# A planned order of instructions that begins earlier and ends later, with a cost model for shared transfers and engines

## The chip, the cores and the metric

The kernel runs on one core of a Trainium2 chip. The metric is the device time of one execution in microseconds (us), as the median of several runs. TensorE (PE) does the matrix products, VectorE (DVE), ScalarE (ACT) and GpSimd (POOL) the elementwise work, and SyncE (SP) issues most of the transfers between memory and the on-chip buffers. Every engine works through its own instructions in the order in which they stand in its program; an instruction that must wait holds up all that stand behind it on its engine. ScalarE issues some transfers too.

## The reference

Two layers over 1024 latent tokens and 256 context tokens of width 1024, in 32-bit floats, then a last RMSNorm. Layer 0 is windowed grouped attention (16 heads, 4 key/value heads, window 128) with a sink logit. Layer 1 is multi-head latent attention: queries from a low-rank projection cq, keys and values from a shared latent ckv, and a rotary part qr and kr. Both outputs are gated.

```python
for i in range(DEPTH):
    shift_x, scale_x, gate_x = adaln(c, ada_w[i], ada_b[i])
    hx = rms_norm(x, norm_g[i]) * (1.0 + scale_x[:, None]) + shift_x[:, None]
    if kind == 0:
        yx, yc = window_gqa(hx, hc, a_w_in[j], a_sink[j], a_w_out[j], ...)
    elif kind == 1:
        yx, yc = latent_attention(hx, hc, b_w_in[j], b_q_norm[j], b_w_uq[j], ...)
    x = x + gate_x[:, None] * yx
return rms_norm(x, final_g)

# in latent_attention
cq, ckv, kr, g = jnp.split(h @ w_in, [...], axis=-1)
q = (rms_norm(cq, q_norm) @ w_uq).reshape(b, n, B_HEADS, B_NOPE + B_ROPE)
kv = (rms_norm(ckv, kv_norm) @ w_ukv).reshape(b, n, B_HEADS, B_NOPE + B_V)
s = (einsum(qn, kn) + einsum(qr, kr)) * scale
yx = (softmax(s) @ v * jax.nn.silu(g)) @ w_out
```

## The kernel before

**Arithmetic.** A 32-bit product is made of three matmuls (`mm3`): each operand is split into a high part, which is a cast (L252), and a low part, which is the difference (L253); the products high-high, high-low and low-high are added in PSUM (L257 to L259). So a weight block reaches TensorE by four steps: a request by SyncE into a staging buffer (`stg`), the cast on ScalarE, the subtraction on VectorE or GpSimd, and the matmuls. Where the table of lines says L184, an instruction went through the recorder described below; its own line is lost.

**Stages.** First come the norms, the conditioning vectors (`AdaLN`, from `ada_w`) and the input projection of layer 0 in ten blocks of 256 columns, `proj_t(bi, gp, c)`, with block bi's weights fetched in four pieces by `fetch` (three at once, the fourth by `second`, since it reuses the first piece's staging buffer). The order within a block is gp 1, 2, 0. Beside the later blocks VectorE sums the products of `ada_w` piece by piece (L479), for the conditioning vectors that TensorE closes at L490. Then the attention of layer 0 runs over `units`. In some of its units (L1124) one of the ten x tiles of layer 1 (128 tokens by 1024, read from `x_d`) is loaded, squared for the norm and scaled ahead of time (`x1_load`, `x1_square`, `x1_scale` with L1093).

Then comes the passage to layer 1. Pairs of x tiles are transposed on TensorE (`turn1`, L1348), evacuated with scale and shift by ScalarE and VectorE (`h1_part`, L1355 and L1356), cast (`h1_top`, L1359) and subtracted (`h1_low`, L1363). Between them TensorE computes ckv and kr of each token tile (`kv_mm`, 288 columns); `kv_rstd` and `kv_post` norm and rotate it. `wq_cut` splits the weights of cq. `krF` holds the rotary keys.

Behind them stand the cq tiles (`cq_tile`, 512 columns in a single matmul each, but two halves in the first tile), then the rotary queries (`qr_tile`: the products on VectorE and GpSimd, their splits, a store), the other queries (`qn_tile`), the weights of keys and values and the gates (`g_tile`). Then the latent attention and the output projection.

**What sets the order.** Up to block 8 and from cq on, each engine's instructions stand in an order that the framework's own scheduler gives. In between, inside `tc.manual_schedule()`, they stand as the kernel emits them. There `Recorder` keeps every operation while `plan.on` is set, and `plan.emit()` puts them out by a list schedule: at each step the engine that can start an operation earliest takes, of its ready ones, that which stood first in the program. The times are those of `Plan.cost`, which gives every operation a duration on its engine and a latency for those who wait for it. Transfers are taken to be independent of one another, and VectorE and GpSimd not to disturb each other.

Of the kernel before, what the change touches and what calls it, by code (L numbers as in the profile page):

```python
# [61 lines left out]


class Plan:


    def __init__(self):
        self.ops = []
        self.on = False
        self.late = 0  # L70
        self.acc = {}

# [9 lines left out]
    @staticmethod  # L82
    def cost(eng, name, out, aps, k):
        n = out.free_size()
        psum = any(a.tensor.name.startswith("PB") for a in aps)
        if name == "dma_start":
            return 0.45, 2.4 + 4 * int(np.prod(out.shape)) / 385e3
        if eng == "tensor":
            return (0.108 if name == "transpose" else 0.0135 + n * 0.000417), 0.45
        if eng == "scalar":  # L90
            return 0.16 + n * 0.000857 + (0.12 if k.get("accum_out") is not None else -0.07 if n > 400 else 0), 0.34
        if eng == "gpsimd":
            if n < 8:
                return 0.59 if ALU.pow in k["alu"] else 0.21, 0.08
            return (0.18 + n * 0.00085 if "copy" in name else 0.19 + n * 0.00215), 0.08
        if name == "tensor_tensor_reduce":
            return 0.14 + n * 0.00105, 0.38
        if name == "reciprocal":
            return 0.1 + n * 0.0065, 0.17
        return (0.07 if psum else 0.03) + n * 0.00106, 0.37  # L100

    def add(self, eng, name, fn, a, k, line):
# [21 lines left out]
        func = a[2] if name == "activation" else None  # L124
        issue = FunctionType(at_line.__code__.replace(co_firstlineno=line), globals())
        self.ops.append((eng, dur, lat, deps, i + self.late, func, lambda: issue(fn, a, k)))

    def emit(self):
# [5 lines left out]
        ready, free, table, end = {}, {}, [None], [0.0] * n  # L134
        open_ = {}
        for i, o in enumerate(self.ops):
            if not left[i]:
                open_.setdefault(o[0], {})[i] = 0.0
        for _ in range(n):
            best = None  # L140
            for e, c in open_.items():
                if not c:
                    continue
                t = max(free.get(e, 0.0), min(c.values()))
                i = min((i for i, r in c.items() if r <= t), key=lambda i: self.ops[i][4])
                if best is None or t < best[0]:
                    best = (t, e, i)
            t, e, i = best
            del open_[e][i]
            _, dur, lat, _, _, func, fn = self.ops[i]  # L150
            if func in (AF.Exp, AF.Tanh, AF.Silu):
                kind = func == AF.Silu
                dur += 1.28 if table[0] not in (None, kind) else 0
                table[0] = kind
            fn()
            free[e] = t + dur
            for u in users[i]:
                left[u] -= 1
                x = t + dur + (0 if self.ops[u][0] == e and lat < 1 else lat)
                end[u] = max(end[u], x)  # L160
                if not left[u]:
                    open_.setdefault(self.ops[u][0], {})[u] = end[u]
# [4 lines left out]
class Recorder:  # L167
# [8 lines left out]
    def __getattr__(self, what):  # L176
# [3 lines left out]

        def call(*a, **k):
            if self.plan.on:
                return self.plan.add(self.name, what, fn, a, k, sys._getframe(1).f_lineno)
            return fn(*a, **k)  # L184

# [4 lines left out]
def kernel(ctx: ExitStack, tc: tile.TileContext, t, out, dbg=None):  # L190
# [842 lines left out]
    for bi, gp, c in order:  # L1033
        plan.on = plan.on or bi >= 8
        next_item()
# [62 lines left out]
    for ui, u in enumerate(units):  # L1098
# [14 lines left out]
        for ci in range(u.m):  # L1113
# [3 lines left out]
            if ci == 0:  # L1117
# [45 lines left out]
    qn = f_at(8, 512)  # L1163
    kvn = f_at(34, 256)
    stg = Ring(F, [30, 32, 64.25], 512)
# [251 lines left out]
    two = turn_two()  # L1417
    x1_square(4)
    h1_two(two)
    h1_two_out(two)  # L1420
    x1_square(5)
    x1_scale(4)
    x1_load(6)
    x1_load(7)
    for _ in last_outproj:
# [10 lines left out]
    for ti in range(NT):  # L1436
        h1_two(two)
        if ti < 5:
            x1_scale(ti + 5)
        if ti:  # L1440
# [3 lines left out]
        h1_two_out(now)  # L1444
        if ti < 4:
            x1_square(ti + 6)
        if ti:
# [56 lines left out]


    NU = 16
    Vq = f_at(34, NT, 4, 64)
# [434 lines left out]
```

## Time and profile before

| what | value |
|---|---|
| median of 3 runs | 1516.65 us (1516.38 to 1517.19) |
| the profiled execution | 1517.31 us |
| its span (first to last instruction) | 1515.5 us |
| granted TensorE clock, mean | 0.995 |
| moved by DMA | 178.93 MB, 118 GB/s |

The span is what the profiler saw on the core; the time of an execution has some 2 us more around it. The profile's page counts busy time of every engine; "idle before" is the time in which an engine stood ahead of an instruction, put down to the semaphore that came last. For an engine that is busy 98% of the time, the few waits are what an order can change.

### The profile page before, as it was taken

Reading aid. Unit: us, or ns where it says so; the run is one execution under the profiler, and the core shown is the slowest. Engines: PE = TensorE matmul, PEld = TensorE weight load, DVE = VectorE, ACT = ScalarE, POOL = GpSimd, SP = SyncE. Lnnn points to the kernel's source line nnn. Section 1 sums busy time; section 2 is a strip of 40 time slices with the busy share of each in tenths; the row PEclk is TensorE's granted clock in tenths of the full one; section 3 lists DMA queues with packets and bytes.
Section 4 is the critical chain, followed back from the end, with each engine's and each line's share of the span. In section 5 each row is a group of like instructions: output and inputs, shape, how many; then the busy total and the mean of one; then the engine's idle time right before and its main releaser. Section 6 shows DMA issues by size and latency. Waiting matters only on the chain.

```text
span 1515.5 us, 24962 instructions
## 1 busy us (share of the span) xinstructions
PE 1483.0 (98%) x9138; PEld 1200.5 (79%) x9138; DVE 954.5 (63%) x1871; ACT 710.3 (47%) x1363; POOL 818.4 (54%) x739
## 2 busy tenths in 40 slices
PE   6999999999999999998999999999999999999998
PEld 4888888788888888888887888677777767876687
DVE  4697689638778888878445103576466556565744
ACT  4421212259888888875333421354345434443422
POOL 2463265346454444456236420588789788789100
PEclk9999999999999999999999999999999999999999
DMA  9555654754343333343125831402212121111442
GB/s 335 162 186 165 192 184 137 235 176 115 122 150 123 93 95 90 95 130 126 43 70 211 258 94 62 113 15 60 63 46 67 46 77 60 46 50 42 156 151 84
DMA packets 128339, 178.93 MB, mean 118 GB/s; under 512 B 11980, under 2 KB 80716, under 8 KB 128216
## 3 DMA queue, kind: packets, MB, share of 16 engines
q1 hardware_dynamic: 123960, 170.93, 36.0%
q10 hardware_dynamic: 4256, 6.40, 1.2%
q8 instruction: 72, 1.18, 0.3%
q14 instruction: 51, 0.42, 0.1%
HBM read 131.13 MB, written 46.15 MB: 117 GB/s over the span
## 4 chain that ended last, share of the span: by engine, by line
PE 48%; POOL 2%; issue 1%; DVE 1%; ACT 0%; DMA 0%; ACTq 0%; POOLq 0%; DVEq 0%
PE PB L184 47%; POOL arena_f L184 1%; DVE arena_f L184 0%; DMA arena_f<-b_w_uq 0%; POOL arena_r L184 0%; ACT arena_f L184 0%; ACT arena_r L184 0%; DVE arena_r L184 0%; DVE arena_r L1363 0%; PE PB L259 0%; PE PB L257 0%; PE PB L258 0%; ACT arena_f L1355 0%; DVE arena_f L1219 0%; ACT arena_f L1186 0%
## 5 line engine op out<-in xcount | busy, mean ns | idle before, releaser
L184 PE MATMUL PB<-arena_r 128*128 128x512 f32 (+4 forms) x5296 | 843.8, 368 | 6.1 <-POOL arena_r L184 3.5
L184 PEld LDWEIGHTS PB<-arena_r 128*128 128x128 f32 (+2 forms) x5296 | 729.3, 187 | 121.8 <-issue 15.9
L184 POOL TENSOR_TENSOR arena_f<-arena_f 128x1024 f32<-128x1024 f32 (+2 forms) x205 | 423.9, 2068 | 147.7 <-ACT arena_f L184 90.5
L184 ACT ACTIVATE arena_f<-PB 128x1024 f32<-128x1024 f32 (+2 forms) x194 | 184.8, 953 | 244.5 <-PE PB L184 237.2
L184 DVE TENSOR_REDUCE krF<-PB 128x1 f32<-128x512 f32 (+1 forms) x324 | 205.9, 680 | 90.9 <-PE PB L184 90.9
L184 POOL TENSOR_TENSOR arena_r<-arena_f,arena_r 128x512 fp32r<-128x512 f32 x93 | 125.7, 1365 | 120.8 <-ACT arena_r L184 117.2
L676 DVE CUSTOM_DVE_ANT_0 arena_f<-PB,arena_f,small 128x256 f32<-128x256 f32 (+1 forms) x288 | 148.1, 525 | 54.5 <-PE PB L670 36.3
L184 PE MATMUL PB<-arena_f 128*64 128x512 f32 x640 | 145.9, 595 | 0.0
L682 ACT ACTIVATE arena_f<-arena_f,small 128x640 f32<-128x640 f32 (+2 forms) x160 | 119.1, 745 | 19.4 <-DVE small L676 17.8
L257 PE MATMUL PB<-arena_r 128*128 128x512 f32 (+2 forms) x336 | 125.3, 373 | 2.8 <-ACT arena_r L252 2.8
L253 DVE TENSOR_TENSOR arena_r<-PB,arena_r 128x512 fp32r<-128x512 f32 (+1 forms) x176 | 116.9, 673 | 15.6 <-ACT arena_r L252 15.0
L258 PE MATMUL PB<-arena_r 128*128 128x512 f32 (+2 forms) x336 | 122.4, 364 | 0.9 <-POOL arena_r L253 0.8
L259 PE MATMUL PB<-arena_r 128*128 128x512 f32 (+2 forms) x336 | 122.1, 363 | 0.0
L184 DVE SCALAR_TENSOR_TENSOR arena_f<-arena_f,small 128x512 f32<-128x512 f32 x100 | 109.8, 1148 | 16.2 <-POOL small L184 14.2
L709 PE MATMUL PB<-arena_r 128*128 128x512 f32 x336 | 118.7, 430 | 0.0
L252 ACT CAST arena_r<-PB 128x512 fp32r<-128x512 f32 (+1 forms) x176 | 99.6, 572 | 31.5 <-PE PB L699 29.9
L699 PE MATMUL PB<-ident,arena_f 128*128 128x128 f32 x672 | 108.5, 272 | 0.1
L184 PEld LDWEIGHTS PB<-arena_f 128*64 128x64 f32 x640 | 44.0, 137 | 79.6 <-issue 79.0
L184 ACT CAST arena_r<-arena_f 128x512 fp32r<-128x512 f32 (+1 forms) x111 | 67.0, 619 | 80.8 <-DVE arena_f L184 35.0
L699 PEld LDWEIGHTS PB<-ident,arena_f 128*128 128x128 f32 x672 | 83.9, 140 | 14.7 <-DVE arena_r L253 0.3
L669 PE MATMUL PB<-arena_r 128*128 128x256 f32 (+1 forms) x288 | 85.3, 312 | 0.3
L184 POOL TENSOR_TENSOR small<-small 128x1 f32<-128x1 f32 (+1 forms) x28 | 14.0, 499 | 130.4 <-ACT arena_f L184 66.9
(127 smaller groups left out, 1576.5 us busy)
## 6 DMA issues: line engine op xcount, KB each, us to landing
arena_f<-ada_w SPq DMA_DIRECT2D x96, 256.0 KB, 3.8
arena_r<-q_d SPq DMA_DIRECT2D x160, 128.0 KB, 2.9
arena_f<-a_w_in SPq DMA_DIRECT2D x40, 256.0 KB, 4.4
arena_f<-x SPq DMA_DIRECT2D x16, 512.0 KB, 6.5
q_d<-arena_f SPq DMA_DIRECT2D x16, 512.0 KB, 2.7
qn_d<-arena_f SPq DMA_DIRECT2D x16, 512.0 KB, 4.8
arena_r<-qn_d SPq DMA_DIRECT2D x16, 512.0 KB, 7.0
arena_f<-b_w_in SPq DMA_DIRECT2D x24, 256.0 KB, 3.1
```

Source lines behind the costliest of these rows:

```text
L184: return fn(*a, **k)
L252: nc.scalar.copy(hi, src)
L253: (lo_eng or nc.vector).tensor_sub(lo, src, hi.bitcast(F32))
L257: nc.tensor.matmul(o, ah, bh, start=first, stop=False)
L258: nc.tensor.matmul(o, al, bh, start=False, stop=False)
L259: nc.tensor.matmul(o, ah, bl, start=False, stop=last)
L669: nc.tensor.matmul(S, q[:, 0], kT[:, g, ko : ko + n], start=True, stop=False)
L676: nc.vector.tensor_tensor_reduce(o, S, mk, -A_SCALE, prev, ALU.add, ALU.min, mx)
L682: nc.scalar.activation(P, P, AF.Exp, bias=nm, scale=-1.0, accum_out=self.den[:, h : h + 1])
L699: nc.tensor.transpose(pt[:, h, :], self.Ps[h][:, ci * 128 : ci * 128 + 128], ident)
L709: nc.tensor.matmul(self.pv, V[:, self.chunks[ci], self.g, :], PT[:, s], start=ci == 0 and s == 0, stop=ci == self.m - 1 and s == 1,)
```

## The change

- The plan begins at `(bi, gp, c) == (9, 1, 1)`, behind the last requests for `a_w_in`, where it began with block 8.
- `plan.emit` stands behind the gates of layer 1, where it stood ahead of cq. So cq, qr, qn, the weights of keys and values and the gates are put in the planned order too. There a TensorE operation may run at most 40 recorded operations ahead of the first one not yet placed (`plan.reach`).
- The times: transfers share one clock (`dma`), each taking its bytes at 385 GB/s plus fixed parts; elementwise operations of VectorE and GpSimd on on-chip buffers slow each other by fixed rates; a SyncE operation that follows another one waits for its latency too.
- Five x tiles are fetched in the attention instead of four (units 24, 27, 30, 33, 36), with other buffers; squares and scalings of the rest move up by one tile.
- The last cq tile is computed in two halves of 256 columns, the second half first.
- An operation that is not planned keeps its own line number as well.

```diff
@@ Plan.cost
-            return 0.45, 2.4 + 4 * int(np.prod(out.shape)) / 385e3
+            return 0.45, 4 * int(np.prod(out.shape)) / 385e3
@@ Plan.add
+        heavy = eng in ("vector", "gpsimd") and "tensor_" in name and "copy" not in name and out.free_size() >= 128
+        heavy = heavy and not any(x.tensor.name.startswith("PB") for x in aps) and (2 if "scalar" in name else 1)
@@ Plan.emit
+                if e == "tensor":
+                    while first < n and (first in done or self.ops[first][0] != e):
+                        first += 1
+                    c = {i: r for i, r in c.items() if i <= first + self.ops[i][7]}
...
+            if e in ("vector", "gpsimd") and func:
+                rate = 0.7 if e == "gpsimd" else 0.35 if func == 1 else 0.65
+                both = max(0.0, big.get("gpsimd" if e == "vector" else "vector", 0.0) - t)
+                dur = min(dur / rate, both + max(0.0, dur - both * rate))
+                big[e] = t + dur
+            if e == "sync" or lat > 0.5:
+                dma = max(dma, t + dur + 1.4) + lat
+                lat = dma + 0.6 - t - dur
...
-                x = t + dur + (0 if self.ops[u][0] == e and lat < 1 else lat)
+                x = t + dur + (0 if self.ops[u][0] == e != "sync" and lat < 1 else lat)
@@ the kernel
-        plan.on = plan.on or bi >= 8
+        plan.on = plan.on or (bi, gp, c) == (9, 1, 1)
...
-    xr = Ring(F, [48, 52, 56, 60, 48, 52, 40, 44, 56, 60], 1024)
-    junk = f_at(36, 512).bitcast(BF16)
+    xr = Ring(F, [48, 52, 56, 60, 34, 48, 40, 44, 56, 60], 1024)
+    junk = f_at(64, 512).bitcast(BF16)
...
-                if ui in (24, 28, 32, 36):
-                    i = ui // 4 - 6
+                if ui in (24, 27, 30, 33, 36):
+                    i = ui // 3 - 8
...
-        for c in range(2) if ti == 0 else (slice(0, 2),):
-            o = ps[:, c * 256 : c * 256 + 256] if ti == 0 else shp(ps, 2, 256)
+        for c in {0: (0, 1), 7: (1, 0)}.get(ti, (slice(0, 2),)):
+            o = ps[:, c * 256 : c * 256 + 256] if ti in (0, 7) else shp(ps, 2, 256)
...
-    x1_load(4)
-    x1_load(5)
+    for i in (5, 6, 7):
+        x1_load(i)
...
-        if ti < 5:
-            x1_scale(ti + 5)
+        if ti < 4:
+            x1_scale(ti + 6)
...
-    plan.emit()
-    in_order.__exit__(None, None, None)
...
+    plan.reach = 40
     for ti in range(8):
         cq_tile(ti)
...
+    plan.emit(tensor=5.0)
+    in_order.__exit__(None, None, None)
```

The code before the planner's new lines is longer by 19 lines at its head, so a line behind it stands 19 lower in the new kernel, up to L1250 or so. Three places of the orders follow, each as it was and as it is.

SyncE's queue at block 9 (`a_w_in` are the projection's weights, `ada_w` the conditioning weights, `g0_d` stored gates), before:

```order
L420 DMA arena_f_65<-a_w_in 128x2x256 x3
L455 DMA arena_f_65<-ada_w 128x512 x2
L469 DMA arena_f_65<-ada_b 1x512
L770 DMA arena_f_65<-a_w_out 128x512
L455 DMA arena_f_65<-ada_w 128x512
L770 DMA arena_f_65<-a_w_out 128x512 x2
L1044 DMA arena_f_65<-mask 128x384
L455 DMA arena_f_65<-ada_w 128x512
L652 DMA arena_f_65<-g0_d_70 128x2x128
L420 DMA arena_f_65<-a_w_in 128x2x256
```

and now:

```order
L439 DMA arena_f_65<-a_w_in 128x2x256 x4
L474 DMA arena_f_65<-ada_w 128x512 x6
L488 DMA arena_f_65<-ada_b 1x512
L474 DMA arena_f_65<-ada_w 128x512 x2
L789 DMA arena_f_65<-a_w_out 128x512 x5
L474 DMA arena_f_65<-ada_w 128x512 x2
L1063 DMA arena_f_65<-mask 128x384
```

The fourth piece of the weights stands directly behind the first three; the ten other requests that stood ahead of it come after it.

VectorE in the passage to layer 1 (L1088 and L1093 are the norm and the scaling of an x tile, L756 and L757 the last rows of layer 0, L1356 the evacuations, L1363 the low halves), before:

```order
L1093 TENSOR_SCALAR arena_f_65<-arena_f_65,small_67 128x1024
L1356 TENSOR_SCALAR arena_f_65<-PB_63,small_67 128x256 x2
L1088 TENSOR_SCALAR small_67<-small_67 128x1 x2
L756 TENSOR_TENSOR arena_f_65<-PB_63,arena_f_65 128x512
L757 TENSOR_TENSOR arena_f_65<-arena_f_65 128x512
L1363 TENSOR_TENSOR arena_r_64<-arena_f_65,arena_r_64 128x512
L756 TENSOR_TENSOR arena_f_65<-PB_63,arena_f_65 128x512
L757 TENSOR_TENSOR arena_f_65<-arena_f_65 128x512
L1356 TENSOR_SCALAR arena_f_65<-PB_63,small_67 128x256 x2
L1093 TENSOR_SCALAR arena_f_65<-arena_f_65,small_67 128x1024
L1363 TENSOR_TENSOR arena_r_64<-arena_f_65,arena_r_64 128x512
L1093 TENSOR_SCALAR arena_f_65<-arena_f_65,small_67 128x1024
```

and now:

```order
L1112 TENSOR_SCALAR arena_f_65<-arena_f_65,small_67 128x1024
L1375 TENSOR_SCALAR arena_f_65<-PB_63,small_67 128x256 x2
L1107 TENSOR_SCALAR small_67<-small_67 128x1
L775 TENSOR_TENSOR arena_f_65<-PB_63,arena_f_65 128x512
L776 TENSOR_TENSOR arena_f_65<-arena_f_65 128x512
L1382 TENSOR_TENSOR arena_r_64<-arena_f_65,arena_r_64 128x512
L775 TENSOR_TENSOR arena_f_65<-PB_63,arena_f_65 128x512
L776 TENSOR_TENSOR arena_f_65<-arena_f_65 128x512
L1375 TENSOR_SCALAR arena_f_65<-PB_63,small_67 128x256 x2
L1112 TENSOR_SCALAR arena_f_65<-arena_f_65,small_67 128x1024
L1382 TENSOR_TENSOR arena_r_64<-arena_f_65,arena_r_64 128x512
L1107 TENSOR_SCALAR small_67<-small_67 128x1
```

The rows look alike, but the tiles differ: the scalings are those of tiles 4, 5 and 6 before and of tiles 5 and 6 now, since tile 4 is done in the attention.

GpSimd at the rotary queries (128x512 rows into `arena_f` are the rope's products and sums, those into `arena_r` low halves of weights), before:

```order
L184 COPY arena_f_65<-krF_68 128x256
L184 TENSOR_TENSOR arena_f_65<-arena_f_65 128x512 x6
L184 TENSOR_TENSOR arena_r_64<-arena_f_65,arena_r_64 128x512
L184 TENSOR_TENSOR arena_f_65<-arena_f_65 128x512
L184 TENSOR_TENSOR arena_r_64<-arena_f_65,arena_r_64 128x512
L184 TENSOR_TENSOR arena_f_65<-arena_f_65 128x512
L184 TENSOR_TENSOR arena_r_64<-arena_f_65,arena_r_64 128x512
L184 TENSOR_TENSOR arena_f_65<-arena_f_65 128x512 x2
L184 TENSOR_TENSOR arena_r_64<-arena_f_65,arena_r_64 128x512 x21
```

and now (L1301 is the product, L1302 the sum):

```order
L1301 TENSOR_TENSOR arena_f_65<-arena_f_65 128x512
L1302 TENSOR_TENSOR arena_f_65<-arena_f_65 128x512
L1301 TENSOR_TENSOR arena_f_65<-arena_f_65 128x512
L1302 TENSOR_TENSOR arena_f_65<-arena_f_65 128x512
L272 TENSOR_TENSOR arena_r_64<-arena_f_65,arena_r_64 128x512 x24
L1555 COPY arena_f_65<-krF_68 128x512
```

The three low halves that stood between the last rope operations now come behind all of them.

More of the change, by code (lines that the diff above doesn't have):

```diff
@@ L61, with at @@
 at_line = lambda fn, a, k: fn(*a, **k)
+def at(line):
+    return FunctionType(at_line.__code__.replace(co_firstlineno=line), globals())
 class Plan:
@@ L70, in __init__ @@
         self.late = 0
+        self.reach = 10 ** 6
         self.acc = {}
@@ L124, in add, with emit @@
         func = a[2] if name == "activation" else None
-        issue = FunctionType(at_line.__code__.replace(co_firstlineno=line), globals())
-        self.ops.append((eng, dur, lat, deps, i + self.late, func, lambda: issue(fn, a, k)))
-    def emit(self):
+        heavy = eng in ("vector", "gpsimd") and "tensor_" in name and "copy" not in name and out.free_size() >= 128
+        heavy = heavy and not any(x.tensor.name.startswith("PB") for x in aps) and (2 if "scalar" in name else 1)
+        self.ops.append((eng, dur, lat, deps, i + self.late, func or heavy, lambda: at(line)(fn, a, k), self.reach))
+    def emit(self, **free):
         n = len(self.ops)
@@ L133, in emit @@
                 users[j].append(i)
-        ready, free, table, end = {}, {}, [None], [0.0] * n
-        open_ = {}
+        table, end, big, dma = None, [0.0] * n, {}, 0.0
+        open_, done, first = {}, set(), 0
         for i, o in enumerate(self.ops):
@@ L149, in emit @@
             del open_[e][i]
-            _, dur, lat, _, _, func, fn = self.ops[i]
+            done.add(i)
+            _, dur, lat, _, _, func, fn, _ = self.ops[i]
             if func in (AF.Exp, AF.Tanh, AF.Silu):
-                kind = func == AF.Silu
-                dur += 1.28 if table[0] not in (None, kind) else 0
-                table[0] = kind
+                dur += 1.28 if table not in (None, func == AF.Silu) else 0
+                table = func == AF.Silu
+            if e in ("vector", "gpsimd") and func:
[6 more added lines that the diff above has]
+                lat = dma + 0.6 - t - dur
             fn()
@@ L181, in call @@
         def call(*a, **k):
+            line = sys._getframe(1).f_lineno
             if self.plan.on:
-                return self.plan.add(self.name, what, fn, a, k, sys._getframe(1).f_lineno)
-            return fn(*a, **k)
+                return self.plan.add(self.name, what, fn, a, k, line)
+            return at(line)(fn, a, k)
         return call
@@ L1163 @@
     qn = f_at(8, 512)
-    kvn = f_at(34, 256)
+    kvn = f_at(66, 256)
     stg = Ring(F, [30, 32, 64.25], 512)
@@ L1417 @@
     two = turn_two()
-    x1_square(4)
+    x1_square(5)
     h1_two(two)
     h1_two_out(two)
[L1421 to L1424, printed above, removed]
+    x1_square(6)
+    x1_scale(5)
     for _ in last_outproj:
@@ L1444 @@
         h1_two_out(now)
-        if ti < 4:
-            x1_square(ti + 6)
+        if ti < 3:
+            x1_square(ti + 7)
         if ti:
```

## The prediction

> **What bounds the kernel now.** I read the page first (busy times, granted clock), then the table of waits for TensorE alone, then busy time by stage, then the timeline at each stage where TensorE stands.
>
> ```profile
> span 1515.5 us, 24962 instructions
> PE 1483.0 (98%) x9138; PEld 1200.5 (79%) x9138; DVE 954.5 (63%) x1871; ACT 710.3 (47%) x1363; POOL 818.4 (54%) x739
> ```
>
> TensorE's own matmuls set the end: of the span only 1515.5 − 1483.0 = 32.5 us are left. A change of order can win no more than its share of these, plus whatever a lowered clock costs. The table of TensorE's waits says whom it stands for (us in total, times, longest):
>
> ```profile
> PE PB L1348 <- DVE arena_f L1093: 4.0, 3, 2.4
> ...
> PE PB L257 <- ACT arena_r L252: 2.8, 1, 2.8
> PE PB L184 <- DVE arena_f L184: 1.8, 2, 1.6
> PE PB L184 <- DVE arena_r L184: 1.5, 2, 0.8
> PE PB L1348 <- ACT arena_f L1355: 1.3, 1, 1.3
> ```
>
> Waits in the opening are left out here; they lie ahead of the point from which the new order reigns. These rows belong to three places, which the busy times by stage show (columns: window, its length, then busy time and count of PE, PEld, DVE, ACT, POOL, granted clock, DMA share, GB/s):
>
> ```profile
> 275.00:295.00 20.00, 16.28 (x57) 12.13 (x56) 13.49 (x14) 6.12 (x11) 6.33 (x5) 0.83 0.93 304
> 295.00:676.00 381.00, 380.63 (x2325) 333.46 (x2324) 282.96 (x862) 299.99 (x722) 183.90 (x325) 1.00 0.39 117
> 676.00:735.00 59.00, 53.47 (x384) 50.41 (x383) 46.68 (x106) 33.16 (x80) 37.41 (x44) 1.00 0.39 133
> 776.00:826.00 50.00, 47.62 (x216) 38.93 (x215) 28.51 (x47) 15.98 (x29) 33.20 (x26) 1.00 0.47 157
> 826.00:1497.00 671.00, 670.31 (x4347) 503.37 (x4346) 355.38 (x507) 264.50 (x351) 422.13 (x232) 1.00 0.29 87
> ```
>
> TensorE idles 3.7 us of 275 to 295 (the last projection block), 5.5 of 676 to 735 (the passage to layer 1) and 2.4 of 776 to 826 (cq to qr to qn). In the attention (295 to 676) it idles 0.4 and behind 826 only 0.7 in 671: there nothing is to be won. So the change is worth what it does at three places, and can cost wherever its order makes TensorE wait anew.
>
> **Place 1: the weights of block 9.** The timeline at 267 to 293 (start, length, engine; in brackets the idle time ahead and its releaser):
>
> ```profile
> 267.14 1.45 SPq L420 DMA_DIRECT2D arena_f<-a_w_in  x3
> 280.66 0.50 SPq L420 DMA_DIRECT2D arena_f<-a_w_in  x1
> 276.08 1.41 POOL L253 TENSOR_TENSOR arena_r<-arena_f,arena_r 128x512 fp32r<-128x512 f32 x1 [6.06 <-ACT arena_r L252]
> 284.54 0.62 ACT L252 CAST arena_r<-arena_f 128x512 fp32r<-128x512 f32 x1 [6.88 <-DMA arena_f<-a_w_in]
> 285.24 1.27 POOL L253 TENSOR_TENSOR arena_r<-arena_f,arena_r 128x512 fp32r<-128x512 f32 x1 [4.35 <-ACT arena_r L252]
> 281.99 0.40 PE L259 MATMUL PB<-arena_r 128*128 128x512 f32 x1
> 285.21 0.50 PE L257 MATMUL PB<-arena_r 128*128 128x512 f32 x1 [2.83 <-ACT arena_r L252]
> 287.15 0.63 PE L259 MATMUL PB<-arena_r 128*128 128x512 f32 x1
> 292.63 0.40 PE L257 MATMUL PB<-arena_r 128*128 128x512 f32 x1
> 286.00:287.00 1.00, 0.44 (x1) 0.44 (x2) 1.00 (x1) 0.00 (x0) 0.51 (x1) 0.50 0.73 230
> DMA to landing us min/median/max: 2.7/4.4/7.9
> ```
>
> Three of the four weight pieces are requested at 267.14, the fourth at 280.66, behind ten other loads in SyncE's queue. It lands at 284.54, ScalarE casts it, POOL makes its low half by 286.51, and TensorE stands. Then the granted clock is 0.50 until 292.3. Between 282.22, when the matmul that began at 281.99 gives way at the undisturbed pace of 0.227 us (12 matmuls from the one listed at 287.15 take 5.1 us at half clock, 0.427 each), and 292.63, fifteen matmuls run. At full pace they take 15 × 0.227 = 3.4; they took 10.4. **The place costs 7.0 us.**
>
> In the new order the fourth request stands directly behind the other three. It reuses the staging buffer of the first piece, so it must wait for POOL's low half of that piece, 276.08 + 1.41 = 277.5, and everything behind it in SyncE's queue waits too. It then goes out at about 277.6, 3.1 us earlier. With the 3.9 us from request to landing that the old one took it lands at 281.5, the cast ends 282.15, the low half 283.45. TensorE needs the high half at 282.2 and the low half at 282.45, so 1.0 us of waiting is left, and no half clock behind it, since the 2.43 us stall of place 2 left the clock at 1.00. Gain 7.0 − 1.0 = 6.0. At the shortest landing of any a_w_in load (2.7 us) nothing waits: 7.0. At the median (4.4) the low half is ready at 283.95: 5.5. The queue is empty by then, which speaks for less than 3.9: I take **6.3**, bounds 5.0 and 7.0.
>
> [...]
>
> What the held queue delays: eight ada_w pieces, the mask, a_w_out, each some 5 us. Their users on VectorE end 18.4 us ahead of the next work there, which waits for TensorE's use of the result:
>
> ```profile
> 313.61 1.40 DVE L495 TENSOR_TENSOR arena_f<-PB,arena_f 1x512 f32<-1x512 f32 x2 [18.42 <-PE PB L490]
> ```
>
> A delay of 5 is hidden three times over. Cost 0; without that cover it would be 5.
>
> **Place 2: the passage to layer 1.**
>
> ```profile
> 685.00:710.00 25.00, 21.98 (x168) 20.99 (x166) 23.70 (x46) 14.90 (x34) 18.91 (x19) 1.00 0.44 146
> 682.40 0.76 DVE L1093 TENSOR_SCALAR arena_f<-arena_f,small 128x1024 f32<-128x1024 f32 x1 [0.66 <-POOL small L1089]
> 690.78 0.99 DVE L1356 TENSOR_SCALAR arena_f<-PB,small 128x256 f32<-128x256 f32 x2
> 691.69 0.74 DVE L1093 TENSOR_SCALAR arena_f<-arena_f,small 128x1024 f32<-128x1024 f32 x1
> 692.49 0.88 PE L1348 MATMUL PB<-ident,arena_f 128*128 128x128 f32 x6 [2.43 <-DVE arena_f L1093]
> 696.76 0.68 DVE L253 TENSOR_TENSOR arena_r<-arena_f,arena_r 128x512 fp32r<-128x512 f32 x1
> 703.08 1.38 DVE L253 TENSOR_TENSOR arena_r<-arena_f,arena_r 128x512 fp32r<-128x512 f32 x1
> 710.33 0.74 DVE L1093 TENSOR_SCALAR arena_f<-arena_f,small 128x1024 f32<-128x1024 f32 x1
> 715.91 0.17 DVE L184 MEMSET krF<- 128x128 f32 x1 [1.61 <-POOL arena_f L184]
> ```
>
> VectorE is the engine here: of 685 to 710 it is busy 23.7 us of 25. TensorE's transposes (L1348) wait for the scaling of the next x tile (L1093), which stands behind evacuations (L1356) and weight splits (L253): the three waits of 4.0 us in the table; the 1.3 us there is the evacuation pair behind a MEMSET of krF that waits 1.6 us for POOL.
>
> The change takes one x tile out of this stretch (it is loaded, squared and scaled in the attention, where TensorE idles 0.4 of 381 us and VectorE has a quarter free): 0.75 us of VectorE. The scaling of tile 5 moves from 691.69 to the place that tile 4's had at 682.40. Behind the last scaling go two of the four splits of cq weights (0.68 and 1.38), the scaling of qn and the MEMSET. Together some 2.8 us of VectorE's work, qn not counted, leave the part in which TensorE waited 4.0 us.
>
> By stall: at 692.49 the scaling is no longer late, but the next evacuation is (the first of the pair at 690.78 ends about 691.3, TensorE comes there about 690.1): 2.4 becomes 1.1, gain 1.3. The other two share the remaining 1.6 of that row: the first (0.6) gives way to an evacuation (0.54, half of the pair's 0.99 and a little), gain 0.1; the second (1.0, for the scaling at 710.33) goes, since that scaling now stands ten places earlier. The 1.3 goes with the MEMSET. Sum 3.8. Lower bound: only the MEMSET's 1.3 is won, less 0.3 for an evacuation that splits now delay; upper: all 5.5 idle less 0.5. I take **3.8**, bounds 1.0 and 5.0.
>
> **Place 3: cq, qr, qn.**
>
> ```profile
> 779.98 0.62 ACT L184 CAST arena_r<-arena_f 128x512 fp32r<-128x512 f32 x1 [1.89 <-DMA arena_f<-b_w_uq]
> 783.46 0.65 PE L184 MATMUL PB<-ident,arena_f 128*128 128x128 f32 x4 [0.82 <-DVE arena_r L184]
> 319.22 0.28 PE L669 MATMUL PB<-arena_r 128*128 128x256 f32 x1
> 319.34 0.28 PE L670 MATMUL PB<-arena_r 128*128 128x256 f32 x1
> 814.27 1.30 POOL L184 TENSOR_TENSOR arena_r<-arena_f,arena_r 128x512 fp32r<-128x512 f32 x1
> 821.08 6.19 PE L184 MATMUL PB<-arena_r 128*128 128x512 f32 x26 [1.56 <-DVE arena_f L184]
> ```
>
> At 783.46 TensorE waits because ScalarE's square of the last cq tile stood behind a cast that waited for a transfer. In the new order the square comes first: 0.8 gained. At 821.08 it waits because VectorE's evacuations of qn stand behind the last rope pair, which stood on POOL behind three weight splits of 1.29; now all rope pairs come first: of 1.6 I take 1.4. The last cq tile is now computed in two halves: 24 matmuls of 512 columns become 48 of 256, nearest rows 319.22 and 319.34 (0.12 apart): 48 × 0.12 = 5.8 against 24 × 0.227 = 5.5, **+0.3**. Sum 0.8 + 1.4 − 0.3 = **1.9** gained, bounds −0.3 and 2.1.
>
> Attention and everything behind 826: order almost unchanged, 0; the new order there could cost up to 1.
>
> **Sum:** 6.3 + 3.8 + 1.9 = 12.0 us. The profiled execution took 1517.31 us (span 1515.5 and 1.8 around it), so 1505.3; it lies 0.66 over the median of the runs shown, 1516.65, so for the median **1504.6**.
>
> **The rivals.**
>
> *VectorE stays the bound in the passage.* What it has to do there is mostly the same; if each wait only turns from a scaling into an evacuation, place 2 gives 0. For it: 23.7 of 25 us busy. Against it: 2.8 us leave. Then 1516.65 − 6.3 − 1.9 = 1508.4.
>
> *The fourth piece lands no earlier.* It is 3.1 us earlier in the queue, and a_w_in loads took up to 7.9 us. At 7.9 it lands at 285.5, as late as now, and place 1 gives nothing: 1510.9. For it: the DMA share is 0.93 in this window. Against it: the loads that filled it stand behind now.
>
> *The clock falls all the same.* A remaining wait near 1 us does little, but if the clock falls for 6.4 us as it did (15 matmuls at 0.427, thus 3.0 lost), 1507.6. For it: the fall came only 0.7 us after the end of an idle stretch of 3 us, so what it counts is not seen. Against it: 2.43 us did nothing at 692.49. [...]
>
> *Slower: SyncE's queue held up in the passage.* The second b_w_uq request now stands ahead of the last x tile's load, and must wait for a staging slot that tile 4's transposes read. That slot comes free about 690. Should it come free only with later transposes, the last x tile comes late: now its load goes out at 695.56 and its scaling is at 710.33.
>
> ```profile
> 695.56 0.42 SPq L1083 DMA_DIRECT2D arena_f<-x_d  x1
> ```
>
> Between request and scaling lie 14.8 us today; a landing of 4.4 (the median quoted for weights), the square and the scaling need some 7, so up to about 703 a delay is free; from there each us costs one, and from 715 on all 12 are eaten. With the slot free at 725, 22 us are lost: 1516.65 − 12 + 22 = 1526.7. Against it: the addresses put the slot's last reader at 690.
>
> *It does nothing measurable:* the moved instructions all sat under waits whose true releaser is another; 1516.
>
> **How the numbers follow.** Chances: the forecast 0.48, VectorE still the bound 0.20, the piece no earlier 0.12, the clock 0.07, nothing 0.06, slower 0.07. What can be told from no change here is 0.2%, 3.0 us: faster 0.87, same 0.06, slower 0.07. The likeliest case by its bounds: 1516.65 − (7.0 + 5.0 + 2.1) = 1502.6 at best, and 1507.4 with places 1 and 2 at 5.5 and 1.9. The range takes in the rivals on that side: **1501 to 1511.5**.
>
> **What would show it.** Right: no wait of TensorE over 1.5 us between 275 and 300 and the granted clock 1.00 there; the transposes' waits (L1348 now) 2 us or less in total; none on VectorE's evacuation at the head of qn; TensorE's idle time down by 9 and its busy time down by 3. Wrong: 0.50 in the clock at 285; a wait for a DMA of a_w_in above 2 us; new waits of TensorE in 735 to 925; an idle SyncE queue in the passage while the last x tile is missing.

## The result and the profile after

The new kernel takes 1503.15 us in the median (1502.81 to 1503.98, 4 runs) against 1516.92 for the one before in the same runs: 0.991 of the time, 95% interval 0.9893 to 0.9927, or 13.8 us less. The profiled execution took 1503.46 us. The page of its profile:

```profile
span 1501.7 us, 24996 instructions
PE 1480.1 (99%) x9162; PEld 1201.6 (80%) x9162; DVE 954.0 (64%) x1871; ACT 708.8 (47%) x1363; POOL 820.1 (55%) x739
```

The span shrank by 13.8 us. TensorE's busy time fell by 2.9, although it runs 24 matmuls more: the half clock at block 9 is gone (the stage's mean was 0.83 before and is 1.00 now). Its idle time fell from 32.5 to 21.6. By stage (the same columns as before; the windows are moved to where the same work lies now):

```profile
275.00:292.00 17.00, 16.95 (x75) 13.51 (x74) 11.30 (x13) 4.64 (x9) 5.98 (x4) 1.00 0.67 233
292.00:668.00 376.00, 375.63 (x2302) 329.23 (x2301) 285.87 (x861) 299.99 (x724) 184.85 (x326) 1.00 0.41 124
668.00:724.00 56.00, 54.84 (x398) 52.65 (x397) 46.53 (x109) 33.10 (x82) 38.10 (x44) 1.00 0.43 147
765.00:815.00 50.00, 49.70 (x235) 41.33 (x234) 31.24 (x50) 18.57 (x34) 38.30 (x29) 1.00 0.61 215
815.00:1484.00 669.00, 668.31 (x4338) 502.01 (x4337) 353.25 (x503) 260.92 (x345) 418.19 (x230) 1.00 0.27 83
```

TensorE idles 0.05 us at block 9 where it idled 3.7, 1.2 in the passage where it idled 5.5, and 0.3 between cq and qn where it idled 2.4. What is left over in the table of its waits:

```profile
PE PB L830 <- DMA arena_f<-ada_w: 8.0, 2, 7.5
PE PB L897 <- POOL arena_r L883: 2.8, 2, 2.4
PE PB L1367 <- DVE arena_f L1375: 1.2, 1, 1.2
...
PE PB L1624 <- DVE arena_r L272: 0.7, 1, 0.7
...
PE PB L277 <- DVE arena_r L272: 0.3, 1, 0.3
```

The first two rows lie in the opening, which the change does not touch. L1367 is the transpose of x tiles (L1348 before): one wait of 1.2 us is left, for an evacuation.

Idle time leaves out a slower clock and a slower first matmul behind a pause (0.50 us at 280.94 in the kernel before, 0.40 for the next one, at 281.28). To divide the gain I set the same matmul, counted from the first, side by side in the two profiles. Block 9 gives −7.1 us, the passage −5.3, cq to qn −2.1. Beside them stand +0.3 in the opening (it differs from profile to profile: its waits for ada_w took 8.0 us here, 7.7 in e8 and 8.9 in e4), +0.2 in the attention and +0.2 at the end: −13.8 in all. One such pair of rows, the conditioning matmuls behind block 9, in the timeline before:

```profile
312.45 1.03 PE L490 MATMUL PB<-arena_f,small 128*1 128x512 f32 x4
```

and now, 6.8 us earlier (7.1 with the opening's 0.3 taken off):

```profile
305.66 1.03 PE L509 MATMUL PB<-arena_f,small 128*1 128x512 f32 x4
```

The place at block 9, from the timeline of the new kernel:

```profile
267.50 10.59 SPq L439 DMA_DIRECT2D arena_f<-a_w_in  x4
280.48 0.62 ACT L271 CAST arena_r<-arena_f 128x512 fp32r<-128x512 f32 x1 [1.73 <-DMA arena_f<-a_w_in]
276.40 6.07 POOL L272 TENSOR_TENSOR arena_r<-arena_f,arena_r 128x512 fp32r<-128x512 f32 x4 [6.06 <-ACT arena_r L271]
```

SyncE has the four requests in one row from 267.50 to 278.09; it sat at the fourth until the first piece's low half was made. The piece landed at 280.48, 2.4 us after the request's end, and GpSimd made the four low halves, nearly without a break, until 282.47. TensorE runs through (16.95 of 17.00 us in the windows above).

### The profile page after: what moved, and what is told of

Its sections match the earlier page's. It is cut to its first block, busy times and chain, and to the rows that moved or that the text cites. A ratio compares the mean times of both kernels' runs of the same rounds, so it can differ in the third digit from the quotient of the medians.

```text
span 1501.7 us, 24996 instructions
## 1 busy us (share of the span) xinstructions
PE 1480.1 (99%) x9162; PEld 1201.6 (80%) x9162; DVE 954.0 (64%) x1871; ACT 708.8 (47%) x1363; POOL 820.1 (55%) x739
## 4 chain that ended last, share of the span: by engine, by line
PE 93%; issue 2%; DMA 2%; DVE 1%; POOL 1%; ACT 1%; POOLq 0%; SPq 0%; DVEq 0%; ACTq 0%
PE PB L276 15%; PE PB L277 15%; PE PB L278 15%; PE PB L1658 13%; PE PB L1681 9%; PE PB L728 5%; PE PB L1624 5%; PE PB L718 5%; PE PB L688 3%; PE PB L689 3%; PE PB L897 1%; PE PB L1692 1%; PE PB L830 1%; PE PB L902 1%; PE PB L747 1%
## 5 line engine op out<-in xcount | busy, mean ns | idle before, releaser
L276 PE MATMUL PB<-arena_r 128*128 128x512 f32 (+2 forms) x1240 | 452.7, 365 | 0.0
L277 PE MATMUL PB<-arena_r 128*128 128x512 f32 (+2 forms) x1240 | 446.4, 360 | 0.3 <-DVE arena_r L272 0.3
L278 PE MATMUL PB<-arena_r 128*128 128x512 f32 (+2 forms) x1240 | 446.0, 360 | 0.0
L1674 POOL TENSOR_TENSOR arena_f<-arena_f 128x1024 f32<-128x1024 f32 x120 | 285.6, 2380 | 8.2
L276 PEld LDWEIGHTS PB<-arena_r 128*128 128x128 f32 x1240 | 234.1, 189 | 44.9 <-issue 9.1
L278 PEld LDWEIGHTS PB<-arena_r 128*128 128x128 f32 x1240 | 234.0, 189 | 34.1
L277 PEld LDWEIGHTS PB<-arena_r 128*128 128x128 f32 x1240 | 234.2, 189 | 32.9 <-DVE arena_r L272 0.7
L1658 PE MATMUL PB<-arena_r 64*128 64x512 f32 (+1 forms) x1600 | 227.4, 395 | 0.0
L1630 DVE TENSOR_REDUCE krF<-PB 128x1 f32<-128x512 f32 (+1 forms) x264 | 167.3, 678 | 79.7 <-PE PB L1624 79.7
L1668 ACT ACTIVATE arena_f<-PB 128x1024 f32<-128x1024 f32 x160 | 164.2, 1026 | 111.9 <-PE PB L1658 83.2
L272 POOL TENSOR_TENSOR arena_r<-arena_f,arena_r 128x512 fp32r<-128x512 f32 (+1 forms) x98 | 133.1, 1373 | 143.3 <-ACT arena_r L271 120.1
L1658 PEld LDWEIGHTS PB<-arena_r 64*128 64x128 f32 (+1 forms) x1600 | 175.6, 186 | 17.0 <-issue 5.2
L272 DVE TENSOR_TENSOR arena_r<-PB,arena_r 128x512 fp32r<-128x512 f32 (+2 forms) x215 | 139.9, 662 | 76.7 <-ACT arena_r L271 75.9
L271 ACT CAST arena_r<-PB 128x512 fp32r<-128x512 f32 (+2 forms) x215 | 119.8, 564 | 110.9 <-PE PB L278 73.8
L1624 PE MATMUL PB<-arena_r 64*128 64x512 f32 (+1 forms) x768 | 111.2, 355 | 0.7 <-DVE arena_r L272 0.7
```

The lines of the kernel that those rows point to most:

```text
L272: (lo_eng or nc.vector).tensor_sub(lo, src, hi.bitcast(F32))
L276: nc.tensor.matmul(o, ah, bh, start=first, stop=False)
L277: nc.tensor.matmul(o, al, bh, start=False, stop=False)
L278: nc.tensor.matmul(o, ah, bl, start=False, stop=last)
L1624: nc.tensor.matmul(bank[:, o : o + n], self.q[r, s, bs], k[r, 0, n0 : n0 + n], start=s == 0, stop=s == 2)
L1630: nc.vector.reduce_max(self.mxp[:, e, b : b + 1, i], bank[:, 0:n], AX.X)
```

## The experiments

In each the time is the median of the runs, and "by place" means the same matmul counted in two profiles. The intervals of the ratios are about ±0.15%, some 2.3 us, so differences of one us rest on the profiles, which are one execution each.

**The begin of the plan, undone and alone.** The new kernel with the old begin:

```diff
-        plan.on = plan.on or (bi, gp, c) == (9, 1, 1)
+        plan.on = plan.on or bi >= 8
```

> The new kernel, but planned from block 8 on as before; the fourth request for the weights of block 9 stands behind nine other requests again, with the new costs in force. Theory (the place of that request in SyncE's queue makes the 7 us, and the planner's later part nothing of them): the stall and the half clock at 282 to 292 come back, 1503.2 + 7 = 1510.2, granted clock 0.50 for about 6 us. Rival (the new costs, which know shared transfers, do it): the request goes out early enough all the same, 1503 to 1505, clock 1.00.

Measured: 1510.51 us, 0.9952 of before (0.9938 to 0.9967). By place: +7.1 at block 9 and nothing anywhere else. The stall and the half clock are back, in its timeline and windows (one us each):

```profile
267.70 1.45 SPq L439 DMA_DIRECT2D arena_f<-a_w_in  x3
281.22 0.47 SPq L439 DMA_DIRECT2D arena_f<-a_w_in  x1
285.82 0.57 PE L276 MATMUL PB<-arena_r 128*128 128x512 f32 x1 [2.92 <-ACT arena_r L271]
```

```profile
285.00:286.00 1.00, 0.18 (x1) 0.18 (x1) 0.00 (x0) 0.85 (x2) 0.16 (x1) 1.00 0.94 278
286.00:287.00 1.00, 0.39 (x1) 0.00 (x1) 0.35 (x1) 0.26 (x1) 1.00 (x1) 0.55 1.11 289
292.00:293.00 1.00, 1.00 (x4) 0.78 (x3) 0.53 (x1) 0.45 (x1) 0.00 (x0) 0.54 1.05 404
293.00:294.00 1.00, 1.00 (x6) 0.81 (x5) 0.62 (x2) 0.20 (x1) 0.00 (x0) 1.00 0.65 242
```

The new costs do not put the request early; only leaving it out of the plan does. (The expectation counts nine requests ahead of it; in the trace they are ten, as in the kernel before.) Then the begin alone, in the kernel before:

> The kernel before, with the later begin of the plan as the only change; the four requests stand in a row. Theory: 7.1 us faster than before, 1509.8, all of it at 275 to 295, the passage to layer 1 as before (5.5 us idle). Rival (without the new costs, loads that were pushed back make a new wait in the attention): 1512 or more, with a new wait of TensorE between 300 and 340.

Measured: 1511.22 us, 0.9956 (0.9939 to 0.9973). By place −7.1 at block 9, as expected, then +0.5 in the attention, +0.2 in the passage, +0.5 between cq and qn. The time lies between theory and rival. In the attention a new wait of 0.3 us for GpSimd stands at 341, at the edge of where the rival put it. The passage waits 1.0 us less for the scalings, but its first stall, which left the clock alone in the kernel before, halved it here (timeline, and windows of one us):

```profile
685.80 1.54 PE L1348 MATMUL PB<-ident,arena_f 128*128 128x128 f32 x6 [2.45 <-DVE arena_f L1093]
685.00:686.00 1.00, 0.20 (x1) 0.20 (x2) 1.00 (x3) 0.66 (x3) 0.85 (x1) 0.89 1.01 410
686.00:687.00 1.00, 1.00 (x7) 1.00 (x6) 1.00 (x2) 0.47 (x1) 0.92 (x2) 0.50 0.33 131
689.00:690.00 1.00, 1.00 (x9) 1.00 (x8) 1.00 (x2) 0.55 (x2) 1.00 (x2) 0.90 0.94 282
```

Counted by place, 1.4 us are lost between the matmuls at 686 and at 689.5. Without this fall of the clock the passage would by estimate (1.4 less the 0.2 above) be some 1.2 us faster than before, and the later parts together about even.

**The end of the plan.** The new kernel, with `plan.emit(tensor=5.0)` and the end of the manual order ahead of cq:

> The new kernel, but the plan ends ahead of cq as before. Theory (the longer plan gives only what was won between cq and qn): 2.1 us slower than the new kernel, 1505.3, with the waits of 0.8 and 1.6 us back. Rival (part of the passage's gain comes from it, since the splits of cq weights and the scaling of qn can be put off only where the plan runs on): 1507 or more, with waits on the transposes of 2 us or more.

Measured: 1505.25 us, 0.9918 (0.9903 to 0.9933). By place +1.2 between cq and qn and +0.2 in the passage, with one wait of TensorE for VectorE of 1.2 us at the head of qn (809.3). The rest of the 2.1 lies in the opening and at block 9 of the profile, 0.9 together, which the edit can't reach. So the longer plan is worth 1.2 there; the wait of 0.8 does not come back. The rival is out: the passage does not need the longer plan.

**The x tiles, undone and alone.** First the new kernel with four tiles and the old buffers, units and squares:

```diff
-                if ui in (24, 27, 30, 33, 36):
-                    i = ui // 3 - 8
+                if ui in (24, 28, 32, 36):
+                    i = ui // 4 - 6
```

> The new kernel with four x tiles fetched in the attention as before, their buffers as before. Theory (tile and order share the passage's 5.3 us, since the tile is 0.75 of some 2.8 us that VectorE loses there): 1.5 to 3 us slower than the new kernel, 1504.7 to 1506.2. Rival A (the tile does it all, because TensorE's first stall is for its scaling): 5 us slower, 1508. Rival B (the order does it all): no more than 0.5 slower.

Measured: 1504.77 us, 0.9915 (0.99 to 0.993). By place +1.3 in the passage. The tile has a share of 1.3 in the 5.3; neither rival holds. Then the five tiles alone, in the kernel before:

> The kernel before, with the five x tiles in the attention and their buffers as the only change. Theory (the tile is worth what its removal cost the new kernel, 1.3 us in the passage): 1 to 2 us faster than before, 1515.1 to 1516.1, with the wait of 1.3 us for the evacuation behind the MEMSET still there, and place 1 unchanged. Rival (the tile's scaling carries the first stall of 2.4 and the others by itself, and in the new kernel the order only repeats it): 3 to 4 us faster.

Measured: 1517.95 us, 1.0006 (0.9997 to 1.0016): nothing, and both expectations miss. Its waits show why:

```profile
PE PB L1348 <- ACT arena_f L1355: 3.3, 4, 0.9
...
PE PB L1348 <- DVE arena_f L1356: 2.0, 2, 1.1
```

The waits for the scaling (L1093: 4.0 us) are gone, and waits for the evacuations (L1355, L1356) have grown from 1.3 to 5.3. With the old times the planner turns one wait into the other. That is the rival of the prediction that gave the passage 0, true for this part alone.

**The planner's times.** The new kernel without the rule that VectorE and GpSimd slow each other:

```diff
-            if e in ("vector", "gpsimd") and func:
-                rate = 0.7 if e == "gpsimd" else 0.35 if func == 1 else 0.65
-                both = max(0.0, big.get("gpsimd" if e == "vector" else "vector", 0.0) - t)
-                dur = min(dur / rate, both + max(0.0, dur - both * rate))
-                big[e] = t + dur
```

> The new kernel without the rule that VectorE and GpSimd slow each other in the planner's times. Theory (that rule lets the planner see VectorE as late as it is in the passage, and so puts splits and the MEMSET behind): 2 to 4 us of the passage's 5.3 come back, 1505 to 1507, place 1 unchanged. Rival (the order follows from the later begin and the tile, and the rule changes nothing that TensorE waits for): 1503 within 0.7.

Measured: 1509.5 us, 0.9952 (0.9935 to 0.9968). By place +5.5 in the passage and nothing behind it: without this rule the whole gain of the passage is gone, more than the 2 to 4 expected, tile and longer plan notwithstanding. Its second stall, in the timeline:

```profile
691.24 1.72 DVE L1377 TENSOR_TENSOR arena_r<-arena_f,arena_r 128x512 fp32r<-128x512 f32 x1
692.88 0.68 DVE L267 TENSOR_TENSOR arena_r<-arena_f,arena_r 128x512 fp32r<-128x512 f32 x1
693.55 0.68 DVE L267 TENSOR_TENSOR arena_r<-arena_f,arena_r 128x512 fp32r<-128x512 f32 x1
694.15 0.53 DVE L1370 TENSOR_SCALAR arena_f<-PB,small 128x256 f32<-128x256 f32 x1
694.72 1.02 ACT L1369 ACTIVATE arena_f<-PB,small 128x256 f32<-128x256 f32 x2 [3.71 <-DVE arena_f L1370]
695.33 0.66 PE L1362 MATMUL PB<-ident,arena_f 128*128 128x128 f32 x4 [1.39 <-ACT arena_f L1369]
```

and the same passage in the new kernel:

```profile
689.10 1.06 ACT L1374 ACTIVATE arena_f<-PB,small 128x256 f32<-128x256 f32 x2
690.26 0.68 DVE L1382 TENSOR_TENSOR arena_r<-arena_f,arena_r 128x512 fp32r<-128x512 f32 x1
691.32 0.98 DVE L1375 TENSOR_SCALAR arena_f<-PB,small 128x256 f32<-128x256 f32 x2
692.75 0.82 PE L1367 MATMUL PB<-ident,arena_f 128*128 128x128 f32 x6
698.23 1.71 DVE L1382 TENSOR_TENSOR arena_r<-arena_f,arena_r 128x512 fp32r<-128x512 f32 x1
```

Without the rule VectorE makes a low half (L1377) and splits (L267) ahead of one evacuation (L1370); ScalarE's pair waits for that one, 3.7 us idle by the profile's releaser, and TensorE waits for ScalarE. With the rule the evacuations stand in pairs here, ScalarE's first, and are done at 692.3, before TensorE comes (the first two of its eight transposes stand ahead of the row shown, at 692.53).

The old price of transfers (the edit also takes out the latency from one SyncE operation to the next, so the two are not told apart):

> The new kernel with the old price of transfers (each by itself, 2.4 us and its bytes) and without the latency from one SyncE operation to the next. Theory (shared transfers matter where a cast waits for a load that the planner thinks landed: at cq to qr): 0.8 to 1.5 us slower, 1504 to 1504.7, with a wait for a square of cq again. Rival (shared transfers carry the passage too, by the x tiles' loads): 3 us or more slower.

Measured: 1504.21 us, 0.9919 (0.9905 to 0.9934). The time is as the theory had it, the place is not: +1.4 in the passage, and −0.5 between cq and qn. The two together are worth about 1 us, in the passage.

**Are the splits what the rule puts off?** A dependency is added, so that VectorE can take a split only once the operation that stands ahead of it in the program is done:

```diff
+        if self.gate is not None and eng == "vector":
+            deps.add(self.gate)
...
+        if c == 0 and i >= 0:
+            plan.gate = len(plan.ops) - 1
         split(wcq[:, c, 0, ks, :], wcq[:, c, 1, ks, :], wq[2 + 4 * c][i], eng)
+        plan.gate = None
```

In the new kernel without the rule:

> The new kernel without the rule of mutual slowing (1509.5 as it was), but with the four splits of the first cq weights held back by a made-up dependency: VectorE may take each only where the program has it, not as filler between earlier evacuations. Theory (the rule wins the passage by putting these splits behind): 3 us or more of the 5.4 come back, 1505 to 1506.5. Rival (the rule wins by how it sets evacuations against one another and against the MEMSET): 1508 or more.

Measured: 1509.13 us, 0.9946 (0.9929 to 0.9963); by place the passage still has +5.4. In the trace three of the four splits have moved behind 711; the first still runs at 689.0, presumably because the operation ahead of it was done early. The stall shown above shrinks from 1.39 to 0.61 us, and other waits make up for it. The theory falls: these three splits are not what the rule wins. In the kernel before with five tiles, where two splits are held (`i >= 2`):

> The kernel before, with five x tiles in the attention (no gain alone) and the third and fourth of those splits held back. Theory (the splits are what the tile's room in VectorE is filled with otherwise): 2 to 4 us faster than the tiles alone, 1513.5 to 1515.5. Rival (the evacuations' own order and the MEMSET bound the passage): within 1 us of the tiles alone, 1517 to 1518.

Measured: 1515.56 us, 0.9992 (0.9983 to 1.0001). By place −1.4 in the passage against the five tiles alone; by the medians it is 2.4 faster, at the edge of the theory's 2 to 4. Splits cost something there, but not the 5. And in the new kernel itself:

> The new kernel with all four splits of the first cq weights held back. Theory (they stand behind already where it matters): within 0.7 us of 1503.2, the wait of 1.2 us for an evacuation stays. Rival (the two that still stand early cost that wait): up to 1.2 faster, 1502.

Measured: 1504.47 us, 0.9917 (0.9902 to 0.9932): +1.2 in the passage, worse than either expectation. Why was not followed up; that work which can't be taken as filler is late elsewhere is a guess.

**The last cq tile in one piece.**

```diff
-        for c in {0: (0, 1), 7: (1, 0)}.get(ti, (slice(0, 2),)):
+        for c in range(2) if ti == 0 else (slice(0, 2),):
```

> The new kernel with the last cq tile in one piece of 512 columns. Theory (24 matmuls fewer, and ScalarE's order alone removed the wait of 0.8): 0.3 us faster, 1502.9. Rival (the halves free the weights' buffer early, and that removed the wait): the 24 matmuls save 0.3 and the wait of 0.8 comes back, 0.5 slower, 1503.7; the trace tells the two apart by TensorE's waits at 760 to 775.

Measured: 1506.15 us, 0.9931 (0.9916 to 0.9946). By place +2.3 between cq and qn, more than both expected. The timeline without the halves:

```profile
769.33 1.67 ACT L271 CAST arena_r<-arena_f 128x512 fp32r<-128x512 f32 x3
771.45 10.91 SPq L379 DMA_DIRECT2D arena_f<-b_w_uq  x7
770.01 0.73 PE L276 MATMUL PB<-arena_r 128*128 128x512 f32 x2 [1.39 <-ACT arena_r L271]
```

and in the new kernel:

```profile
763.53 1.67 ACT L271 CAST arena_r<-arena_f 128x512 fp32r<-128x512 f32 x3
765.65 12.55 SPq L379 DMA_DIRECT2D arena_f<-b_w_uq  x7
```

The weights of qr go where the second half of the cq weights lies. The last tile's matmuls on that half come first now, so ScalarE casts the qr weights 5.8 us earlier and the next requests follow 5.8 us earlier (5.1 when the 0.7 by which the profile without the halves is late already is taken off). In one piece TensorE waits for the casts themselves.

**The bound on how far TensorE runs ahead.** The new kernel without `plan.reach = 40`:

> The new kernel without the bound of 40 operations on how far TensorE may run ahead. Theory (the bound is what keeps TensorE from taking matmuls out of a tile that waits, and it costs or gives little, since TensorE waits 0.3 us there): within 1 us, 1502.5 to 1504.2. Rival (without it TensorE takes far tiles early, banks and engines behind it run late): 1505 or more, with new waits between 725 and 830.

Measured: 1505.59 us, 0.9923 (0.9909 to 0.9938). By place +3.2 between cq and qn, with a wait of 2.0 us for a cast of the qr weights: the rival holds. In its timeline ScalarE's first casts of the qr weights stand here:

```profile
768.77 1.15 ACT L271 CAST arena_r<-arena_f 128x512 fp32r<-128x512 f32 x2
```

In the new kernel they begin at 763.53. Without the bound TensorE starts the last tile's halves at 737.9 instead of 755.8, while other tiles still need the weights, so no half comes free early. The 3.2 are not all the order's: the clock fell behind this wait, too.

```profile
769.45 0.89 PE L276 MATMUL PB<-arena_r 128*128 128x512 f32 x2 [1.97 <-ACT arena_r L271]
769.00:770.00 1.00, 0.55 (x2) 0.45 (x3) 1.00 (x4) 1.00 (x3) 0.18 (x1) 0.93 0.00 0
770.00:771.00 1.00, 1.00 (x6) 0.86 (x5) 1.00 (x3) 0.93 (x2) 0.75 (x1) 0.50 0.00 0
773.00:774.00 1.00, 1.00 (x5) 0.77 (x5) 0.34 (x1) 0.96 (x2) 0.00 (x0) 0.86 0.31 92
```

At half clock (0.50) for 3.4 us TensorE loses, by estimate, up to 1.7. The fastest run of this kernel, at 1504.57, is 1.4 slower than the new kernel; the profiled one, at 1506.28, is the slowest.

None of the kernels is faster than the new one. Two things were not tried: the rule of mutual slowing by itself in the kernel before, and `tensor=5.0`, which makes `plan.emit` take TensorE as busy up to 5 us.

## Why the prediction was right, and where not

The forecast was 1504.6 with a range of 1501 to 1511.5; 1503.15 lies in it, and the likeliest case came about. Step by step:

- **Block 9** (predicted 6.3, bounds 5.0 and 7.0): 7.1. The mechanism was right in each part: the wait for the first low half, the request 3 us earlier, no half clock. The term was small because the landing was put at 3.9 us behind the begin of the request; now the request begins at 277.7, when SyncE has issued nothing for 8.8 us, and the cast starts at 280.48, 2.8 us later. The shortest landing of an a_w_in load, 2.7 us, for which the prediction works out a gain of 7.0, was nearer than the 3.9. That the remaining stall would not halve the clock was put down to the 2.43 us that had not done so; e2 shows that this was no safe ground (2.45 us, halved), but no stall was left here. (The half clock before ran from 285.7 to 292.5 by the windows, so it came 0.5 us behind the stretch of idle time, not 0.7.) The delayed ada_w pieces cost nothing, as worked out: there is no wait of TensorE behind block 9 in the new kernel.
- **The passage** (predicted 3.8, bounds 1.0 and 5.0): 5.3, over the upper bound. (The four gains of the working add up to 3.7, not 3.8.) Two steps of the working failed. "Behind the last scaling go two of the four splits … Together some 2.8 us of VectorE's work … leave" was taken as the cause; e9 shows that splits held back win nothing without the rule. And the tile, which the prediction gave the first gain of 1.3, is worth that only within the new order (1.3 in e4, nothing in e5). What wins is the order that the planner finds once it knows how slow VectorE is beside GpSimd (a subtraction of 0.68 us takes 1.71 in the rows of the last section; e6: 5.5); at the one stall shown it has the evacuations ahead of low halves and splits. The prediction saw the order change but costed only the moved work. Which of the many swapped rows of VectorE and ScalarE carries how much was not tried singly and stays open.
- The evacuation that was to remain at 692 (1.1) remains: 1.2 in the table of waits. The other four stalls, of which 0.5 was to remain at 701, are gone.
- **cq to qn** (predicted 1.9, bounds −0.3 and 2.1): 2.1. The size was right, in part by luck, since the reason was in good part wrong. The wait of 0.8 was laid to ScalarE's square behind a cast, and the halves of the last tile were costed as +0.3 and no gain. The halves carry 2.3 (e8), the bound on running ahead 3.2 (e11, up to 1.7 of it by the clock), the longer plan 1.2 (e3): each of them is needed, so their prices can't be added up. The prediction overlooked which region of the on-chip buffer the halves set free. That the 1.6 of the rope pairs is won by the longer plan agrees with e3, where a wait of 1.2 for VectorE comes back.
- **The rivals.** VectorE as the bound did not come, but it is what the tile alone does. The clock did not fall at block 9 (1.00 in the windows). The fourth piece did land earlier, by 4.1 us. The held queue of SyncE in the passage cost nothing: no wait for the last x tile.

## What to carry to other kernels

When a list schedule is worked out from a cost model, a rule that one engine slows another can be worth more than the work that is moved: 5.5 us here against 1.3 for the tile. It changes what is taken as filler ahead of something another engine waits for. Requests for weights at the edge of a plan deserve a place by hand: here one request behind ten others cost 7.1 us, of which some 3 came from the clock (fifteen matmuls at 0.427 us each where the full pace is 0.227). And a buffer that is shared by two stages can be freed half by half, in the order in which the next stage's weights go in.

## What the runs showed of the hardware

Behind block 8 the half clock followed stalls of 2.83 us (before), 2.92 (e1), 3.08 and 3.01 (e5 and e10), but also one of 2.45 (e2) and one of 1.97 (e11). It did not follow 2.43 us (before, the same place as in e2) nor 1.39 (e8, where the granted clock is 1.00 in the windows from 768 to 782). So in these profiles the length of a stall alone does not tell whether the clock falls, and two equal ones end differently. By windows of one us the half clock lasted 6.8 us at block 9 (in e1, by the 0.55 and 0.54 shown there, from 286.1 to 292.9) and 3.4 in e2 (685.8 to 689.2) and e11 (769.9 to 773.3). At block 9, where it lasted twice as long, a second stall (0.8 us in e1, until 287.2) lies behind the first. The shortest stall that it followed is the 1.97 us of e11.

A subtraction of 128 by 512 on VectorE takes 0.68 us with little beside it (at 690.26 in the new kernel) and 1.71 (at 698.23) where GpSimd runs a subtraction from 697.78 to 699.39:

```profile
697.78 1.61 POOL L1382 TENSOR_TENSOR arena_r<-arena_f,arena_r 128x512 fp32r<-128x512 f32 x1
```

GpSimd's own takes 1.61 there against 1.28 in the kernel before at 811.78, where VectorE idles. A scaling of VectorE was running when it started (0.97 long, against 0.74 at 710.33 in the kernel before, where GpSimd idles; a cast of GpSimd ran beside it until 697.70):

```profile
697.28 0.97 DVE L1112 TENSOR_SCALAR arena_f<-arena_f,small 128x1024 f32<-128x1024 f32 x1
```

The GpSimd subtraction at 814.27 in the kernel before, which the prediction shows, started with VectorE idle and took 1.30 us, although a VectorE one came second:

```profile
814.99 1.12 DVE L184 TENSOR_TENSOR arena_f<-arena_f 128x512 fp32r<-128x512 f32 x1 [4.14 <-ACT arena_f L184]
```

In both cases VectorE ends some 0.55 us behind GpSimd (699.94 against 699.39, 816.11 against 815.57). Its subtraction, the second of each pair, took longer there (1.71 and 1.12 against 0.68); of the two GpSimd ones one kept its time (1.30) and one did not (1.61). The evacuations, which read PSUM, take about the same in either neighbourhood: in e6 0.54 us at 688.98, beside a GpSimd subtraction (687.83 to 689.64), and 0.54 at 695.77, where GpSimd idles. Such pairs are what the planner's rule of mutual slowing stands for, though its fixed rates do not depend on who started first.
